# Two mixture-of-experts layers on one core: row fetches issued two experts ahead, parameter pieces queued behind them, gathers ahead of additions

## The chip, the cores and the metric

The kernel runs on one core of a Trainium2 chip. The metric is device microseconds (us) of one execution, and the figure that counts is the median of several executions. The engines are TensorE (PE, with its weight loads as PEld), VectorE (DVE), ScalarE (ACT), GpSimd (POOL) and SyncE (SP). Each has its own queue of instructions and works through it in order. SP, ACT and POOL also issue DMAs, and an issue is an instruction of their queue.

## The reference, cut to what matters

Two layers are computed over 512 tokens of 1024 numbers. Each layer has a mixer and then a mixture of 16 experts of which every token takes two. For every expert the tokens that chose it are collected, and with x those rows:

```python
hb = jax.nn.silu(xb @ w1[e]) * (xb @ w3[e])
return hb @ w2[e]
...
ys = ys * buf_gate[:, None]
out = jax.ops.segment_sum(ys, buf_tok, num_segments=T + 1)[:T]
```

The second layer's mixer has a state-space part (S5). Its small parameters go through exponentials, sines, cosines and a complex division before they are used; that work depends on nothing in the first layer, so it can be done while the first layer's experts run.

## The kernel before

Every float32 product is made as three products of a split operand: `split_half` (L335) takes a weight piece of 128x1024, ACT copies it to a rounded high part `wh` (L342) and DVE subtracts to get the low part `wl` (L343). PE then multiplies high by high, high by low and low by high (`mm3`, L346, lines 348 to 350). There are four buffers for `wh` and four for `wl` (L136), so that the splits run at most four ahead of PE.

`moe` (L1308) loops over the experts e = 0 to 15 (L1357). One turn of the loop holds, in this order of tracing: the products with W1 of expert e, the products with W2 of expert e - 1, the transposes of the rows of expert e + 1 (L1389), the products with W3 of expert e, and `expert_mid` of expert e (L1396), which applies the activation and transposes again. Each of the three weights is 4 MB and comes in four loads of 1 MB on SP, into a ring of buffers whose keys stand in `order`. In the first layer three keys leave that ring from expert 4 on (L1358 to 1359): the two `sx` buffers take the next layer's S5 parameters and `wx` gives its space to the work tiles of their preparation. When the preparation is over, `wx` goes back to the ring (L1405 to 1407).

The rows of experts 0 and 1 are gathered by products. Those of experts 2 to 15 are fetched by an indirect DMA from DRAM, issued on POOL: `fetch` (L1172, the DMA at L1174). At L1370 the rows of expert e + 1 are fetched in turn e, and they are transposed by PE in that same turn at L1256. The tile `xr` with the rows, and the transposed `hx` tiles, come from one ring of eight buffers.

The preparation of the S5 parameters is the generator `s5_params` (L479). In the first layer it is called with POOL as its engine and `two` = 1, at the end of turn 4 (`PREP`, L39, L1397 to 1400), after four small loads on the ACT queue (`s5_loads`, L459). Each `next` at L1403 traces the operations up to the next `yield`, at the end of one turn; there are nine yields for `two` = 1, so that the last operations are traced at the end of turn 13. One operation of it is a reciprocal on DVE (L545); all others are on POOL. `issue_after(ins)` sets only an order of issue: what the block traces on the engine of `ins` stands behind `ins` in that engine's queue. `self.mid` holds an ACT and a DVE instruction (L1258 and L1259), so the two `issue_after` at L1402 bind none of the POOL operations. The order within a queue is otherwise set by a planner when the kernel is built: it goes through the instructions by priority (by default the order of tracing, `high_priority` moves a block forward) and takes those that it holds to be ready, by its own estimate of when buffers and operands are there.

After the last expert `collect` (L1445) brings each token's two expert outputs together. For each of four groups of 128 tokens it issues two indirect gathers on POOL (L1452), into a buffer of the weight ring that is free again, and adds the two (L1457): the first 512 columns on DVE, the other 512 on POOL. `combine` (L1533) adds the sums to the accumulators by a product with the identity (L1543), beside the products for the last two experts' rows (`add_known`, L1432, and L1545). The fifth free buffer serves the last normalisation's scales (L268) or a scratch tile.

Of the kernel before, what the change touches and what calls it, by code (L numbers as in the profile page):

```python
# [21 lines left out]
NT = T // P  # L22
D = 1024
KD = D // P
DEPTH = 2
NE = 16
# [97 lines left out]
class Kernel:  # L124
# [354 lines left out]
    def s5_params(self, sp, sm, V, two):  # L479
# [4 lines left out]
        t = lambda nm, n=8: sp.tile([P, n], F32, name=nm, tag=nm)  # L484
# [11 lines left out]
        xm = t("xm", 64)  # L496
        V.tensor_tensor(v3(xm, 8), x[:, :, None].to_broadcast([P, 8, 8]),
                        mult[:, None, 0:8].to_broadcast([P, 8, 8]), OP.mult)
        mag = v3(self.poly_exp(sp, xm, 64, V), 8)
        at = 8 * NP * 16  # L500
        mag8 = self.s5c[:, at:at + 8]
# [8 lines left out]
        r = t("r", N)  # L510
        self.stt(V, r, k, -c1, af, OP.mult, OP.add)
        self.stt(V, r, k, -c2, r, OP.mult, OP.add, sp)
        V.tensor_scalar(r, r, 0.25, None, OP.mult)
        if two == 2:
            yield
        x2, s, cm = t("x2", N), t("s", N), t("cm", N)
        V.tensor_tensor(x2, r, r, OP.mult)
        V.tensor_scalar(s, x2, 1.0 / 362880, None, OP.mult)
        for f in (-1.0 / 5040, 1.0 / 120, -1.0 / 6):
            self.stt(V, s, s, f, x2, OP.add, OP.mult)  # L520
        self.stt(V, s, s, 1.0, r, OP.add, OP.mult)
        V.tensor_scalar(cm, x2, -1.0 / 3628800, None, OP.mult)
        for f in (1.0 / 40320, -1.0 / 720, 1.0 / 24, -0.5):
            self.stt(V, cm, cm, f, x2, OP.add, OP.mult)
        u = t("x2", N)
        for _ in range(2):
            self.stt(V, u, cm, 1.0, s, OP.add, OP.mult)
            self.stt(V, cm, s, -2.0, s, OP.mult, OP.mult)
            V.tensor_scalar(s, u, 2.0, None, OP.mult)
# [5 lines left out]
        V.tensor_tensor(L[:, 0], L[:, 0], mag, OP.add)  # L535
        V.tensor_tensor(L[:, 1], mag, v3(s, NT_)[:, :, 0:8], OP.mult)
        V.tensor_scalar(L[:, 2], L[:, 1], -1.0, None, OP.mult)
        l1, li = t("l1"), L[:, 1, :, 0]
        V.tensor_scalar(l1, L[:, 0, :, 0], -1.0, None, OP.add)
        d0, d1, n0, n1 = t("d0"), t("d1"), t("n0"), t("n1")  # L540
# [26 lines left out]
        for h in range(4):  # L567
# [3 lines left out]
            c = [cx[r][:, hs, 0:1, :].to_broadcast([P, *f]) for r in range(2)]  # L571
# [599 lines left out]

    def fetch(self, r, e):  # L1172
        t = self.keep.tile([P, D], F32, tag="hx", name="xr", bufs=8)[0:CAP]
        self.nc.gpsimd.indirect_dma_start(out=t, out_offset=None, in_=self.x_dram[:, :],  # L1174
                                          in_offset=bass.IndirectOffsetOnAxis(ap=r["idx"][e], axis=0))
        return t

    def places(self, r, pool):
# [129 lines left out]
    def moe(self, l, lg, nb, rs):  # L1308
        tc, nc, a = self.tc, self.nc, self.a
        W1, W3, W2 = (a[n][l] for n in ("moe_w1", "moe_w3", "moe_w2"))  # L1310
        Y = self.y_dram
        with tc.high_priority():
            self.keep_awake(WARM, self.asked)
            r = self.route(lg, self.hi)
        with self.pool("mw") as mw, ExitStack() as spare:
            self.wx = spare.enter_context(self.pool("wx"))

            def mk(e):
                def load(w, u):
                    key = order.pop(0)  # L1320
                    order.append(key)
                    return self.load(w[e, u * 256:(u + 1) * 256, :].rearrange("(k p) f -> p k f", p=P), (2, 1024),
                                     *slot(key))
                return load

            def slot(key):
                if key == "wx":
                    return self.wx, 1
                return (self.sx[int(key[2])], 1) if key[:2] == "sx" else bufs[key]
            bufs = dict(mr=(self.mr, 2), raw=(self.raw, 2), rows=(self.rows, 3))  # L1330
            order = ORDER.split()
# [22 lines left out]
                    self.gathered((ps[k][:, 0:256], ps[k][:, 256:]), nxt, k, 2, P)  # L1354
            pend = prep = None
            y = []
            for e in range(NE):  # L1357
                if e == PREP and l + 1 < self.layers:  # L1358
                    order[:] = [k for k in order if k[1] != "x"]
                if e == 1:  # L1360
                    with tc.issue_after(self.mid[1]):
                        self.places(r, self.hi)
                g = max(i for i, (a, n) in enumerate(GROUPS) if e >= a)
                at = e - GROUPS[g][0]
                if g == 0:
                    x = [[t[k // 4][:, k % 4, at * P:at * P + CAP] for k in range(KD)] for t in nxt]
                else:
                    x = cur
                if 0 < e < NE - 1:
                    xr = self.fetch(r, e + 1)  # L1370
                with ExitStack() as after:
                    if e == 0:
                        after.enter_context(tc.issue_after(r["dv"]))
                        after.enter_context(tc.issue_after(r["ex"]))
                    a1 = self.expert_in(W1, x, mk(e), ("pj", "pj"), ready if e == 0 else ())
                self.calm = False
                if e == 0:
                    with tc.issue_after(self.chosen):
                        self.gates(r, self.hi)
                        self.slots(mw, r, 0)  # L1380
                if e == NE - 1:
                    half = self.expert_out(mw, W2, pend, mk(e - 1), None, range(2))
                elif pend is not None:
                    y13 = self.keep.tile([P, D], F32, tag="hx", name="y", bufs=8) if e == NE - 2 else None
                    self.expert_out(mw, W2, pend, mk(e - 1), Y[(e - 1) * CAP:e * CAP, :], y=y13, gate=r["gate"][e - 1])
                if at == 0 and e < NE - 2:
                    A = self.slots(mw, r, g + 1)
                if 0 < e < NE - 1:
                    cur = self.transpose_split(xr, self.hx(KD * CAP), self.hx(KD * CAP), "zo", False)  # L1389
                if e == NE - 2:  # L1390
                    self.rest(A, r, mw)
                    self.overflow(l, r, mw, Y, y13[:, 0:T])
                a3 = self.expert_in(W3, x, mk(e), ("b", "b"))
                if e == NE - 1:
                    self.expert_out(mw, W2, pend, mk(e - 1), lambda ps: y.append(self.last_y(ps, 0)), range(2, 4), half)
                pend = self.expert_mid(mw, a1, a3)  # L1396
                if e == PREP and l + 1 < self.layers:  # L1397
                    spare.close()
                    sp = spare.enter_context(self.pool("s5p"))
                    prep = self.s5_params(sp, self.s5_loads(l + 1), nc.gpsimd, 1)  # L1400
                if prep:
                    with tc.issue_after(self.mid[0]), tc.issue_after(self.mid[1]):  # L1402
                        done = next(prep, 0) == 0  # L1403
                    if done:
                        prep = spare.close()  # L1405
                        self.wx = spare.enter_context(self.pool("wx"))
                        order.append("wx")
            self.cmb = []
            for c in range(NT - 1):
                self.cmb.append([self.bank(("pj", "b", "oz"[n])[c], "cmb") for n in range(2)])  # L1410
# [34 lines left out]
    def collect(self, r, Y, slots):  # L1445
        nc, tc = self.nc, self.tc
        self.acc = []
        ts = [pool.tile([P, 2048], F32, tag="raw", name="yg", bufs=n) for pool, n in slots]
        for c in range(NT):
            yg = ts[c][:, 0:D], ts[c][:, D:]  # L1450
            for j in range(2):
                nc.gpsimd.indirect_dma_start(out=yg[j], out_offset=None, in_=Y[:, :],  # L1452
                                             in_offset=bass.IndirectOffsetOnAxis(ap=r["pos"][:, j, c:c + 1], axis=0))
            with tc.issue_after(self.cut[1]):
                for i, eng in enumerate((nc.vector, nc.gpsimd)):
                    sl = slice(i * 512, (i + 1) * 512)
                    eng.tensor_tensor(yg[0][:, sl], yg[1][:, sl], yg[0][:, sl], OP.add)  # L1457
            self.acc.append(yg[0])
            self.rt[c] = yg[1]
# [143 lines left out]
```

## Time and profile before

| | us |
|---|---|
| median of 3 runs | 2251.75 |
| lowest and highest run | 2241.91, 2252.71 |
| the profiled execution | 2255.18 |
| its span, first to last instruction | 2253.4 |
| busy PE | 2120.9 (94%) |
| busy DVE | 1532.0 (68%) |
| busy ACT | 1229.7 (55%) |
| busy POOL | 445.4 (20%) |

The mean granted TensorE clock over the span is 0.965. The experts of the first layer run from about 505 to 1125 us of the span, those of the second from about 1638 to 2231 us. A busy PE is not a PE at its peak: matmuls are pipelined, and a product of 512 columns follows the one before it after about 0.23 us where its own row shows about 0.39 us. The time 2255.18 is that of the execution that the trace shows; times worked out from its rows are set against it, and it stands 3.43 us above the median.

### The profile page before, as it was taken

To read this page: it belongs to the slowest core of one execution; us is meant where nothing else is said; L and a number is where in the kernel's file an instruction comes from. 1 tells how busy PE (TensorE), PEld (TensorE's weight loads), DVE (VectorE), ACT (ScalarE), POOL (GpSimd) and SP (SyncE) were. 2 spreads that over 40 slices of the span, in tenths; PEclk is the share of its full clock that TensorE was granted. 3 is DMA by queue.
4 is the path that set the end of the run, shared out by engine and by line. 5 is a ranking of instruction groups with operands and counts; after the bars stand their busy time and mean duration, and the time that the engine had idled before them with its cause. 6 is when DMAs were issued, how large, how long until landed. Compare 5 with 4: busy or idle time off the path is not lost. (4 is left out here: it accounts for less than half of the span.)

```text
span 2253.4 us, 27509 instructions
## 1 busy us (share of the span) xinstructions
PE 2120.9 (94%) x10180; PEld 1564.4 (69%) x10181; DVE 1532.0 (68%) x1986; ACT 1229.7 (55%) x1548; POOL 445.4 (20%) x535
## 2 busy tenths in 40 slices
PE   7899999989993999998999999999899999999987
PEld 5678778876772666665667686888777776666654
DVE  8453533379993888887763435433699998888877
ACT  3333123237883777876643331223378887777763
POOL 5310231130069010000260101511310000000004
PEclk9999999999997999999999889999999999999999
DMA  6121365339995899998831112453289999999973
GB/s 195 46 74 52 105 206 179 118 124 349 373 344 185 319 360 380 367 378 319 319 124 57 39 64 64 165 182 122 103 320 386 385 389 351 380 366 382 367 302 125
DMA packets 192461, 533.16 MB, mean 237 GB/s; under 512 B 18545, under 2 KB 72433, under 8 KB 192306
## 3 DMA queue, kind: packets, MB, share of 16 engines
q1 hardware_dynamic: 173312, 476.69, 57.2%
q0 software_dynamic: 8032, 28.84, 3.8%
q10 hardware_dynamic: 10962, 25.67, 3.4%
q8 instruction: 84, 1.38, 0.2%
q14 instruction: 71, 0.58, 0.1%
HBM read 501.14 MB, written 27.00 MB: 234 GB/s over the span
## 5 line engine op out<-in xcount | busy, mean ns | idle before, releaser
L343 DVE TENSOR_TENSOR wl<-raw,wh 128x1024 fp32r<-128x1024 f32 x850 | 1026.6, 1242 | 392.0 <-ACT wh L342 366.8
L342 ACT CAST wh<-raw 128x1024 fp32r<-128x1024 f32 x872 | 895.8, 1050 | 426.3 <-PE e L350 150.1
L349 PE MATMUL e<-wl,hx 128*96 128x512 f32 x1024 | 408.2, 399 | 7.1 <-DVE wl L343 7.1
L350 PE MATMUL e<-wh,hx 128*96 128x512 f32 x1024 | 407.8, 398 | 0.0
L348 PE MATMUL e<-wh,hx 128*96 128x512 f32 x1024 | 383.6, 398 | 11.5 <-PEq L1480 11.3
L348 PE MATMUL pjf<-hx,wh 128*128 128x512 f32 x608 | 244.4, 402 | 4.5 <-DVE v L215 4.5
L350 PE MATMUL pjf<-hx,wl 128*128 128x512 f32 x608 | 243.7, 401 | 3.0 <-DVE wl L343 3.0
L349 PE MATMUL pjf<-hx,wh 128*128 128x512 f32 x608 | 244.5, 402 | 0.5 <-DVE hx L216 0.4
L349 PEld LDWEIGHTS e<-wl,hx 128*96 128x96 f32 x1024 | 166.9, 163 | 81.2 <-DVE wl L343 14.9
L348 PEld LDWEIGHTS e<-wh,hx 128*96 128x96 f32 x1024 | 166.7, 163 | 80.3 <-issue 12.5
L350 PEld LDWEIGHTS e<-wh,hx 128*96 128x96 f32 x1024 | 166.9, 163 | 66.5
L349 PE MATMUL e<-wl,gh 128*96 128x512 f32 x512 | 203.0, 396 | 5.0 <-DVE wl L343 4.2
L350 PE MATMUL e<-wh,gl 128*96 128x512 f32 x512 | 201.2, 394 | 2.6 <-DVE gl L1259 2.6
L348 PE MATMUL e<-wh,gh 128*96 128x512 f32 x512 | 180.2, 394 | 0.0
L1174 POOL DMA_INDIRECT xr<-xd,idx x28 | 43.2, 1543 | 675.5 <-PE tx L1256 498.4
L348 PEld LDWEIGHTS pjf<-hx,wh 128*128 128x128 f32 x608 | 115.6, 190 | 33.1 <-DVE v L215 5.7
L350 PEld LDWEIGHTS pjf<-hx,wl 128*128 128x128 f32 x608 | 115.5, 190 | 29.9 <-DVE wl L343 3.4
L349 PEld LDWEIGHTS pjf<-hx,wh 128*128 128x128 f32 x608 | 115.4, 190 | 28.9 <-DVE hx L216 1.6
L349 PEld LDWEIGHTS e<-wl,gh 128*96 128x96 f32 x512 | 82.6, 161 | 44.7 <-DVE wl L343 12.1
L350 PEld LDWEIGHTS e<-wh,gl 128*96 128x96 f32 x512 | 82.5, 161 | 36.2 <-DVE gl L1259 3.5
L348 PEld LDWEIGHTS e<-wh,gh 128*96 128x96 f32 x512 | 82.5, 161 | 35.3
L949 POOL TENSOR_TENSOR mg<-mg,gsg 128x512 f32<-128x512 f32 x32 | 42.8, 1342 | 212.2 <-DVE gsg L948 187.9
(500 smaller groups left out, 2787.0 us busy)
## 6 DMA issues: line engine op xcount, KB each, us to landing
raw<-in_moe_w_dram SPq DMA_DIRECT2D x384, 1024.0 KB, 7.5
raw<-in_w_in_dram SPq DMA_DIRECT2D x44, 1024.0 KB, 5.3
yd<-y ACTq DMA_DIRECT2D x28, 384.0 KB, 6.0
raw<-in_w_out_dram SPq DMA_DIRECT2D x8, 1024.0 KB, 5.5
yd<-zr ACTq DMA_DIRECT2D x14, 384.0 KB, 4.4
row<-hd POOLq DMA_DIRECT2D x8, 512.0 KB, 7.4
rawu<-in_w_up_c_dram SPq DMA_DIRECT2D x8, 512.0 KB, 3.4
xd<-row POOLq DMA_DIRECT2D x8, 512.0 KB, 3.1
```

Of the source, the lines that this page charges most:

```text
L342: self.cut = (nc.scalar.copy(hv, v).ins, (eng or nc.vector).tensor_tensor(lv, v, hv.bitcast(F32), OP.subtract).ins)
L343: (eng or nc.vector).tensor_tensor(lv, v, hv.bitcast(F32), OP.subtract).ins)
L348: mm(out, lh, rh, start=start, stop=False)
L349: mm(out, lh, rl, start=False, stop=False)
L350: mm(out, ll, rh, start=False, stop=stop)
L949: nc.gpsimd.tensor_tensor(mg[m], mg[m], sg, OP.add)
L1174: self.nc.gpsimd.indirect_dma_start(out=t, out_offset=None, in_=self.x_dram[:, :], in_offset=bass.IndirectOffsetOnAxis(ap=r["idx"][e], axi ...
```

## The change

`fetch` now keeps its DMA instruction in `self.fetched`. It is called at the end of the transposes of turn e, under `high_priority`, for expert e + 2, where before it was called at the head of turn e for expert e + 1. The preparation gets more yields for `two` = 1 (fifteen in place of nine), and `step` is called twice in a turn, after the W2 products and at the end, so that the last piece is traced in the middle of turn 12. What a step traces on POOL is queued behind the latest fetch in place of the two `mid` instructions, and its DVE reciprocal is bound to nothing. In `collect` all eight gathers are traced before the first addition. The yield that used to be taken for `two` = 2 alone is now taken for both, and the preparation of the first layer (`two` = 2, on DVE) yields where it did.

```diff
--- before.py
+++ after.py
@@ -496,6 +496,8 @@
         xm = t("xm", 64)
         V.tensor_tensor(v3(xm, 8), x[:, :, None].to_broadcast([P, 8, 8]),
                         mult[:, None, 0:8].to_broadcast([P, 8, 8]), OP.mult)
+        if two == 1:
+            yield
         mag = v3(self.poly_exp(sp, xm, 64, V), 8)
         at = 8 * NP * 16
         mag8 = self.s5c[:, at:at + 8]
@@ -511,19 +513,22 @@
         self.stt(V, r, k, -c1, af, OP.mult, OP.add)
         self.stt(V, r, k, -c2, r, OP.mult, OP.add, sp)
         V.tensor_scalar(r, r, 0.25, None, OP.mult)
-        if two == 2:
-            yield
+        yield
         x2, s, cm = t("x2", N), t("s", N), t("cm", N)
         V.tensor_tensor(x2, r, r, OP.mult)
         V.tensor_scalar(s, x2, 1.0 / 362880, None, OP.mult)
         for f in (-1.0 / 5040, 1.0 / 120, -1.0 / 6):
             self.stt(V, s, s, f, x2, OP.add, OP.mult)
         self.stt(V, s, s, 1.0, r, OP.add, OP.mult)
+        if two == 1:
+            yield
         V.tensor_scalar(cm, x2, -1.0 / 3628800, None, OP.mult)
         for f in (1.0 / 40320, -1.0 / 720, 1.0 / 24, -0.5):
             self.stt(V, cm, cm, f, x2, OP.add, OP.mult)
         u = t("x2", N)
         for _ in range(2):
+            if two == 1:
+                yield
             self.stt(V, u, cm, 1.0, s, OP.add, OP.mult)
             self.stt(V, cm, s, -2.0, s, OP.mult, OP.mult)
             V.tensor_scalar(s, u, 2.0, None, OP.mult)
@@ -535,6 +540,8 @@
         V.tensor_tensor(L[:, 0], L[:, 0], mag, OP.add)
         V.tensor_tensor(L[:, 1], mag, v3(s, NT_)[:, :, 0:8], OP.mult)
         V.tensor_scalar(L[:, 2], L[:, 1], -1.0, None, OP.mult)
+        if two == 1:
+            yield
         l1, li = t("l1"), L[:, 1, :, 0]
         V.tensor_scalar(l1, L[:, 0, :, 0], -1.0, None, OP.add)
         d0, d1, n0, n1 = t("d0"), t("d1"), t("n0"), t("n1")
@@ -1171,8 +1178,9 @@
 
     def fetch(self, r, e):
         t = self.keep.tile([P, D], F32, tag="hx", name="xr", bufs=8)[0:CAP]
-        self.nc.gpsimd.indirect_dma_start(out=t, out_offset=None, in_=self.x_dram[:, :],
-                                          in_offset=bass.IndirectOffsetOnAxis(ap=r["idx"][e], axis=0))
+        at = bass.IndirectOffsetOnAxis(ap=r["idx"][e], axis=0)
+        self.fetched = self.nc.gpsimd.indirect_dma_start(out=t, out_offset=None, in_=self.x_dram[:, :],
+                                                         in_offset=at).ins
         return t
 
     def places(self, r, pool):
@@ -1354,6 +1362,17 @@
                     self.gathered((ps[k][:, 0:256], ps[k][:, 256:]), nxt, k, 2, P)
             pend = prep = None
             y = []
+
+            def step():
+                nonlocal prep
+                if prep is None:
+                    return
+                with tc.issue_after(self.fetched):
+                    done = next(prep, 0) == 0
+                if done:
+                    prep = spare.close()
+                    self.wx = spare.enter_context(self.pool("wx"))
+                    order.append("wx")
             for e in range(NE):
                 if e == PREP and l + 1 < self.layers:
                     order[:] = [k for k in order if k[1] != "x"]
@@ -1366,8 +1385,6 @@
                     x = [[t[k // 4][:, k % 4, at * P:at * P + CAP] for k in range(KD)] for t in nxt]
                 else:
                     x = cur
-                if 0 < e < NE - 1:
-                    xr = self.fetch(r, e + 1)
                 with ExitStack() as after:
                     if e == 0:
                         after.enter_context(tc.issue_after(r["dv"]))
@@ -1383,10 +1400,14 @@
                 elif pend is not None:
                     y13 = self.keep.tile([P, D], F32, tag="hx", name="y", bufs=8) if e == NE - 2 else None
                     self.expert_out(mw, W2, pend, mk(e - 1), Y[(e - 1) * CAP:e * CAP, :], y=y13, gate=r["gate"][e - 1])
+                step()
                 if at == 0 and e < NE - 2:
                     A = self.slots(mw, r, g + 1)
                 if 0 < e < NE - 1:
                     cur = self.transpose_split(xr, self.hx(KD * CAP), self.hx(KD * CAP), "zo", False)
+                if e < NE - 2:
+                    with tc.high_priority():
+                        xr = self.fetch(r, e + 2)
                 if e == NE - 2:
                     self.rest(A, r, mw)
                     self.overflow(l, r, mw, Y, y13[:, 0:T])
@@ -1398,13 +1419,7 @@
                     spare.close()
                     sp = spare.enter_context(self.pool("s5p"))
                     prep = self.s5_params(sp, self.s5_loads(l + 1), nc.gpsimd, 1)
-                if prep:
-                    with tc.issue_after(self.mid[0]), tc.issue_after(self.mid[1]):
-                        done = next(prep, 0) == 0
-                    if done:
-                        prep = spare.close()
-                        self.wx = spare.enter_context(self.pool("wx"))
-                        order.append("wx")
+                step()
             self.cmb = []
             for c in range(NT - 1):
                 self.cmb.append([self.bank(("pj", "b", "oz"[n])[c], "cmb") for n in range(2)])
@@ -1446,11 +1461,12 @@
         nc, tc = self.nc, self.tc
         self.acc = []
         ts = [pool.tile([P, 2048], F32, tag="raw", name="yg", bufs=n) for pool, n in slots]
-        for c in range(NT):
-            yg = ts[c][:, 0:D], ts[c][:, D:]
+        ygs = [(t[:, 0:D], t[:, D:]) for t in ts]
+        for c, yg in enumerate(ygs):
             for j in range(2):
                 nc.gpsimd.indirect_dma_start(out=yg[j], out_offset=None, in_=Y[:, :],
                                              in_offset=bass.IndirectOffsetOnAxis(ap=r["pos"][:, j, c:c + 1], axis=0))
+        for c, yg in enumerate(ygs):
             with tc.issue_after(self.cut[1]):
                 for i, eng in enumerate((nc.vector, nc.gpsimd)):
                     sl = slice(i * 512, (i + 1) * 512)
```

## Rows read from the trace of the kernel before

**Rows 1.** The page, span in 40 slices: the granted TensorE clock in tenths.
```profile
PEclk9999999999997999999999889999999999999999
```

**Rows 2.** Waits of PE: who waited for whom, us in total, times, longest.
```profile
PE tx L1256 <- DMA xr<-xd,idx: 37.8, 1, 37.8
...
PE cmb L1543 <- POOL yg L1457: 8.8, 2, 5.4
```

**Rows 3.** Timeline of POOL, first layer, 597 to 790 us: start, length, operation, idle before.
```profile
597.69 2.17 POOL L1174 DMA_INDIRECT xr<-xd,idx  x1 [32.64 <-PE tx L1256]
637.87 0.28 POOL L443 TENSOR_SCALAR pe_xc<-small 128x8 f32<-128x8 f32 x1 [38.02 <-DMA small<-in_small_dram]
...
708.79 0.19 POOL L502 COPY s5c<-pe_o 128x8 f32<-128x8 f32 x1
...
729.33 0.53 POOL L580 TENSOR_SCALAR s5c<-s5c 128x128 f32<-128x128 f32 x1
730.03 1.02 POOL L1174 DMA_INDIRECT xr<-xd,idx  x1 [0.16 <-issue]
...
790.02 1.07 POOL L551 TENSOR_TENSOR zr<-n,d 128x8 f32<-128x8 f32 x1 [47.16 <-DVE d L545]
```

**Rows 4.** Line L1174 over the whole span: fetches from issue to landing.
```profile
DMA to landing us min/median/max: 4.0/8.1/11.2
```

**Rows 5.** Stretches of the first layer: busy us of each engine, PEclk, DMA share.
```profile
core 0: us, PE busy (x) PEld busy (x) DVE busy (x) ACT busy (x) POOL busy (x), PEclk, DMA share, GB/s
637.80:696.00 58.20, 58.20 (x273) 41.03 (x271) 54.37 (x53) 47.33 (x54) 54.70 (x57) 1.00 1.01 370
696.00:735.00 39.00, 1.24 (x15) 1.18 (x14) 3.58 (x4) 1.75 (x3) 34.81 (x72) 0.56 0.28 103
735.00:770.00 35.00, 35.00 (x154) 24.52 (x153) 29.03 (x30) 25.52 (x28) 0.91 (x1) 0.95 0.83 299
840.00:875.00 35.00, 34.12 (x158) 23.65 (x157) 30.19 (x31) 27.07 (x32) 1.28 (x1) 1.00 1.00 379
```

**Rows 6.** Transposes of fetched rows, experts 5, 7, 15, then 5, 15 of layer two.
```profile
L1256 PE MATMUL tx<-cs,xr x8: 244/246/247, 661.1 to 661.7; 96*128 96x96 f32 x8
...
L1256 PE MATMUL tx<-cs,xr x8: 243/246/247, 770.8 to 771.4; 96*128 96x96 f32 x8
...
L1256 PE MATMUL tx<-cs,xr x8: 243/244/246, 1041.5 to 1047.6; 96*128 96x96 f32 x8
...
L1256 PE MATMUL tx<-cs,xr x8: 244/246/247, 1794.5 to 1795.1; 96*128 96x96 f32 x8
...
L1256 PE MATMUL tx<-cs,xr x4: 244/246/248, 2134.8 to 2137.8; 96*128 96x96 f32 x4
```

**Rows 7.** Groups of DVE: splits at 637 to 696, then at 1731 to 1790 us.
```profile
L343 DVE TENSOR_TENSOR wl<-raw,wh 128x1024 fp32r<-128x1024 f32 x42 | 51.3, 1230 | 4.0 <-ACT wh L342 3.1
...
L343 DVE TENSOR_TENSOR wl<-raw,wh 128x1024 fp32r<-128x1024 f32 x42 | 50.9, 1222 | 4.1 <-ACT wh L342 3.6 <-DMA raw<-in_moe_w_dram 0.2
```

**Rows 8.** Timeline of POOL at the end of each layer: gathers and additions.
```profile
1112.42 7.30 POOL L1457 TENSOR_TENSOR yg<-yg 128x512 f32<-128x512 f32 x1 [5.24 <-DMA yg<-yd,pos]
...
1132.73 0.93 POOL L1452 DMA_INDIRECT yg<-yd,pos  x1 [0.31 <-issue]
...
2202.85 8.72 POOL L1452 DMA_INDIRECT yg<-yd,pos  x1 [0.15 <-issue]
...
2216.99 1.26 POOL L1457 TENSOR_TENSOR yg<-yg 128x512 f32<-128x512 f32 x1 [4.16 <-DMA yg<-yd,pos]
...
2222.15 0.94 POOL L1452 DMA_INDIRECT yg<-yd,pos  x1 [0.30 <-issue]
```

**Rows 9.** Timeline of PE at the end of each layer: the products that waited.
```profile
1128.10 1.22 PE L1543 MATMUL cmb<-yg,cs 128*128 128x512 f32 x1 [5.37 <-POOL yg L1457]
...
2218.30 1.13 PE L1543 MATMUL cmb<-yg,cs 128*128 128x512 f32 x2 [3.39 <-POOL yg L1457]
```

**Rows 10.** Timeline of DVE at 789.7 us: the reciprocal between two splits.
```profile
789.74 0.19 DVE L545 RECIPROCAL d<-d 128x8 f32<-128x8 f32 x1
```

## The prediction

> **What bounds the kernel now.** I read the whole page first. TensorE is busy for 94% of the span, so time is gained only where PE stands, and the row of the granted clock has one slice of 7 in the first layer's experts [rows 1]. Next I asked for PE's waits: one wait of 37.8 us, of the row transposes for an indirect DMA, is far longer than any other, and it occurs once in 28 fetches; the second to note is 8.8 us in two waits for additions on POOL [rows 2]. Then I read POOL's timeline around the long wait [rows 3]. POOL issues the fetch for expert 5 at 597.69, waits until 637.87 for the S5 loads, and runs preparation without a break to 729.86. Only then comes the fetch for expert 6, at 730.03. PE needed these rows at 696.4, since it went on at 734.20 after its 37.8 us. The fetch's buffer had long been free: in this layer a fetch otherwise goes right behind the transposes one expert earlier, which were those of expert 5, at 661.1 [rows 6]. So the block on POOL made it late, not memory, and the DMA share of 0.28 in the stretch says the weights were waiting too [rows 5].
>
> The second layer has the same experts and no preparation; it is the cleanest comparison at hand. From the transposes of expert 5's rows to those of expert 15's it takes 2134.8 - 1794.5 = 340.3 us, and the first layer 1041.5 - 661.1 = 380.4 us [rows 6]. The difference, 40.1 us, is what one block on POOL costs.
>
> **The fetches.** Fourteen fetches per layer stay fourteen; they move one expert ahead on POOL's queue, past two preparation pieces each, and no queue gets more DMAs. Fetch 6 is now traced in turn 4, ahead of the preparation, which must queue behind it. Its wait of 37.8 us goes. With it goes the clock's fall: while PE stood the granted clock was 0.56, and over the next 35 us it was 0.95 against 1.00 later [rows 5], in all 35 x 0.05 = 1.75 us of PE's work. Sum: 39.5 us, against 40.1 by the comparison of the layers.
>
> What is late next? Without the wait expert 7's transposes come at 770.8 - 39.5 = 731.3 [rows 6]. Fetch 7 can have two pieces ahead of it, the first two. These end with the copy at 708.79, and in the kernel before operations of later pieces ran among them [rows 3], so they end no later now. Fetch 7 then issues by 709 and lands 8.1 us later, 11.2 at worst [rows 4]: by 721, 10 us early. The pieces after it have about 20 operations or fewer between fetches; at 54.70 us for 57 operations, 0.96 us each beside busy splits [rows 5], that is under 20 us of an expert's 34 us (340.3 / 10). I cost them at nothing; if that cover went, each us beyond it would be a us of PE.
>
> The preparation's work itself, some 125 operations, is the same and now lies beside PE for its whole length. Does it slow the splits? DVE's split took 1230 ns with POOL's block beside it and 1222 ns in the second layer without [rows 7]; 8 ns on 42 splits is 0.3 us, and PE was busy for all 58.20 us of that stretch [rows 5]. So I take nothing. The other way round POOL does pay: 0.96 us an operation beside the splits, 34.81 / 72 = 0.48 us while PE and DVE stood [rows 5]. The Trainium skill says more (SBUF — State Buffer, "SBUF: two separate sides"): a DVE operation with two SBUF inputs and a GpSimd operation exclude each other for the whole instruction, whichever starts first. By that rule the splits should lose too, up to 125 x 0.48 = 60 us of DVE over eight experts, an estimate; by the rows it is POOL alone that waits, and the sum stays.
>
> `wx` returns to the ring one and a half turns earlier. More room ahead can only help; the smaller ring gives the first layer no later expert that is slower (from expert 7 to 15, 270.7 / 8 = 33.8 us each, the second layer's 34.0) [rows 6], so I take nothing.
>
> **The reciprocal.** It loses its order behind `mid` and can stand earlier in DVE's queue, where it waits for POOL's operations of the piece before it, which in turn stand behind the fetch for expert 9. Behind the reciprocal in DVE's queue are the splits, and PE runs on four of these: 34 / 24 = 1.4 us each, 5.6 us. Before, it cost 0.19 us between two splits [rows 10], and POOL waited 47.16 us for it, which cost nothing [rows 3]. No row shows DVE waiting for it. From below it costs nothing; it can't gain. From above: the two pieces behind that fetch have 15 operations, 15 x 0.96 = 14.4 us, less PE's 5.6: 9 us. I take 1, near the lower end, since the three products that it needs depend on the loads alone and are the first that POOL finds ready.
>
> **The gathers.** PE stood 5.37 us in the first layer and 3.39 in the second for POOL's addition of the second token group [rows 9], which came behind the first addition, stretched from some 1.26 us to 7.30 in the first layer, and behind a gather issue of 8.72 us in the second [rows 8]. With the gathers ahead, the second group's data is there sooner and both waits can go: from above 8.8 us of gain. From below: if POOL holds to all eight gathers first, the first two additions stand behind the last gather, whose buffer is freed by the last weights. That was issued by 1133.66 in the first layer and by 2223.09 in the second [rows 8]; with two additions of 1.26 us each, PE would go on at 1136.2 instead of 1128.1 and 2225.6 instead of 2218.3, a loss of 8.1 + 7.3 us. Both gathers were late because additions stood ahead of them, so the lower end is too dark. I take 3 us of gain for the first layer, whose buffers also come free earlier with `wx` back in the ring at another place, and 1 for the second, where no buffer changes.
>
> The Trainium skill names a trap here (SBUF — State Buffer, "SBUF: two separate sides"): a DMA issued on GpSimd can't get its descriptors written while DVE holds the shared port. The 8.72 us issue, beside splits, agrees with it; other issues of 0.93 us beside splits do not [rows 8]. By that rule the second layer's later gathers would be stretched again and its gain would be nil.
>
> **Sum.** 37.8 + 1.75 - 1 + 3 + 1 = 42.5 us. From the profiled execution's 2255.2 that gives 2212.7; the median stands 3.4 lower, so 2209.
>
> **Rivals.**
> (a) The reciprocal and the gathers both turn out near their bad ends: 39.5 - 9 - 15.4 = 15 us are left, 2237; half of that, 2224, is likelier. For it: in-order queues, no row that shows either. Against: one stall of each kind only.
> (b) The change doesn't do what it says: a fetch is late all the same, since POOL's pieces stand ahead of fetch 7 with only 10 us to spare. If the loads for the preparation land 10 + x later, x is lost; at the 38 us of now, 2252, no change. Against: the loads come in turn 4 as before, and the order behind a fetch is fixed.
> (c) Slower, by one mechanism: the reciprocal on DVE. If the planner puts it at the place where the whole preparation could begin, and POOL gets to its operands only at the end of some 92 us (637.87 to 729.86) [rows 3], DVE stands 92 us and PE 92 - 5.6 = 86: 2252 - 39.5 + 86 = 2298. It decides from a wait of 45 us (39.5 + 5.6), where all the gain is gone. Against: its operands need the loads only, and stand behind one fetch, not behind all pieces.
>
> **Chances.** Forecast 0.80, with 2198 to 2220 as its own span; (a) 0.10, still faster; (b) 0.06, of which 0.05 ends within 0.5% and 0.01 faster; (c) 0.04. A measurement of this kernel tells about 0.5%, 11 us, from no change. So faster 0.91, same 0.05, slower 0.04. For the range: the lower end is all gains, 40.1 + 8.8 = 48.9 below 2251.75, 2203, and 5 more because the runs before spread 10 us downwards; the upper end takes in the larger part of (a), 2232. That leaves out (b), (c) and the rest of (a).
>
> **What would show it.** The fetch row of PE's waits gone, and no slice of 7 in the clock row before 1000 us; from expert 5's transposes to expert 15's some 340 us in the first layer; POOL's preparation in clumps between fetches over about seven experts; the waits of L1543 shorter than 5.37 and 3.39 us. The prediction is wrong if a transpose still waits for `xr`, if DVE shows a wait of tens of us before L545, or if the split row rises above 1.23 us with PE waiting on L343.

## The result, and the profile after

The kernel after takes 2215.64 us, the median of 8 runs (2207.34 to 2233.51), the kernel before 2252.16 us in 8 runs beside it (2237.64 to 2255.02). The ratio is 0.987, with a 95% interval of 0.9832 to 0.9908, wholly below 1: the kernel is 1.3% faster, inside the range, 6.6 us above the forecast. The profiled execution took 2214.86 us, with a span of 2213.1 and a mean clock of 0.976 (before 2255.18, 2253.4 and 0.965).

The long wait for the fetched rows [rows 2] is gone from PE's waits, which now begin so:

```profile
PE e L349 <- DVE wl L343: 14.7, 31, 2.0
...
PE cmb L1559 <- POOL yg L1473: 7.6, 2, 6.1
```

The first row is the wait for a VectorE split: in the kernel before 11.3 us in 26 waits, the longest 0.6; now 14.7 us, with one of 2.0. The clock row has lost its slice of 7 [rows 1]:

```profile
PEclk9988999999999999999999999999999999999999
```

POOL's timeline (start, length, operation, idle before) shows fetch 6 ahead of the preparation, and fetches 7 and 8 between its pieces, where one block stood before [rows 3]:

```profile
633.70 0.91 POOL L1182 DMA_INDIRECT xr<-xd,idx  x1 [27.83 <-PE tx L1264]
643.96 0.28 POOL L443 TENSOR_SCALAR pe_xc<-small 128x8 f32<-128x8 f32 x1 [9.35 <-DMA small<-in_small_dram]
...
695.02 1.07 POOL L504 COPY s5c<-pe_o 128x8 f32<-128x8 f32 x1
696.26 2.04 POOL L1182 DMA_INDIRECT xr<-xd,idx  x1 [0.17 <-issue]
...
724.68 2.02 POOL L1182 DMA_INDIRECT xr<-xd,idx  x1 [0.16 <-PE e L350]
```

The row transposes of experts 5 and 15, in the first layer and then in the second, answer to [rows 6]:

```profile
L1264 PE MATMUL tx<-cs,xr x8: 244/246/247, 667.2 to 667.8; 96*128 96x96 f32 x8
...
L1264 PE MATMUL tx<-cs,xr x8: 243/244/246, 1013.6 to 1019.7; 96*128 96x96 f32 x8
...
L1264 PE MATMUL tx<-cs,xr x8: 244/246/247, 1755.5 to 1756.1; 96*128 96x96 f32 x8
...
L1264 PE MATMUL tx<-cs,xr x8: 243/244/246, 2095.7 to 2101.9; 96*128 96x96 f32 x8
```

From expert 5 to expert 15, which I call the stretch, the first layer takes 346.4 us (380.4 before) and the second 340.2, as before. So 34.0 us came back and 6.1 are still lost (346.36 - 340.23 by the timeline's hundredths). The lag over the second layer is 0.3 us at expert 9, 2.7 at 10, 5.0 at 11, 6.1 at 12, and then stays: it arises between 798 us, where expert 9's transposes start, and 912, where expert 12's do.

The layers' ends: from expert 15's transposes to the next layer's first product it is 119.3 us (117.1 before), and from those of the second layer to the last instruction 117.4 (118.6). PE's waits at the first combine answer to [rows 9]:

```profile
1099.97 2.08 PE L1559 MATMUL cmb<-yg,cs 128*128 128x512 f32 x2 [6.09 <-POOL yg L1473]
...
2177.94 1.12 PE L1559 MATMUL cmb<-yg,cs 128*128 128x512 f32 x2 [1.49 <-POOL yg L1473]
```

The span fell by 40.3 us: 34.0 in the stretch, 1.3 at the second layer's end, less 2.2 at the first layer's. Nearly all of the other 7.2 lies in the two mixers, which the change doesn't touch: the first is 6.0 us longer (its clock from 100 to 200 us is 0.86, was 0.93), the second 13.5 shorter (0.98, was 0.95). Among all the kernels run, expert 2's transposes come anywhere from 555.2 to 565.1 us, with nothing altered ahead of them. What the change itself does is thus 32 to 33 us (the second layer's 1.3 may not be its own), and single runs are compared below by the stretch, which in the second layer is 340.1 to 340.4 us in every kernel run.

### The profile page after: what moved, and what is told of

Read it like the earlier page. It is cut to its first block, busy times and chain, and to the rows that moved or that the text cites. A ratio compares the mean times of both kernels' runs of the same rounds, so it can differ in the third digit from the quotient of the medians.

```text
span 2213.1 us, 27508 instructions
## 1 busy us (share of the span) xinstructions
PE 2114.7 (96%) x10178; PEld 1557.3 (70%) x10181; DVE 1545.0 (70%) x1986; ACT 1230.4 (56%) x1548; POOL 505.0 (23%) x535
## 5 line engine op out<-in xcount | busy, mean ns | idle before, releaser
L343 DVE TENSOR_TENSOR wl<-raw,wh 128x1024 fp32r<-128x1024 f32 x850 | 1042.3, 1261 | 345.5 <-ACT wh L342 310.6
```

Source lines behind the costliest of these rows:

```text
L343: (eng or nc.vector).tensor_tensor(lv, v, hv.bitcast(F32), OP.subtract).ins)
```

## The experiments

All edits are to the kernel after, except where said. The whole time is a median for before, after, best and chain_late, and one run for the others.

| kernel | stretch, layer 1 | end, layer 1 | whole us |
|---|---|---|---|
| before | 380.4 | 117.1 | 2252.2 |
| after | 346.4 | 119.3 | 2215.6 |
| undo_queue | 381.3 | 120.0 | 2243.7 |
| undo_early | 346.1 | 119.3 | 2213.4 |
| undo_pieces | 349.0 | 118.4 | 2215.9 |
| queue_alone | 358.2 | 117.6 | 2232.5 |
| undo_gathers | 347.0 | 119.7 | 2218.4 |
| wide_on_vector | 342.1 | 122.3 | 2217.8 |
| wide_twice | 350.7 | 119.6 | 2229.5 |
| wide_cut | 358.6 | 119.7 | 2227.6 |
| cut_chain | 340.9 | 119.2 | 2220.1 |
| wx_late | 347.4 | 117.1 | 2215.1 |
| best | 342.0 | 116.9 | 2207.0 |
| chain_late | 341.0 | 117.4 | 2208.0 |

### Which part carries the gain

**undo_queue.**
```diff
-                with tc.issue_after(self.fetched):
+                with tc.issue_after(self.mid[0]), tc.issue_after(self.mid[1]):
                     done = next(prep, 0) == 0
```


> The kernel after with the pieces held behind the two middle steps, as before, and not behind the last fetch; fetches still two experts ahead, pieces still small. POOL is then given fetches 2 to 5, the whole preparation (some 125 operations), and fetch 6 behind it. Theory QUEUE (what costs is the fetch standing behind the preparation on POOL, wherever the code writes it): fetch 6 near 730 us, a wait of TensorE of 30 to 40 us for it, a stretch of 376 to 384. Rival AHEAD (two experts of distance are what carries the gain): 346 to 350.

381.3 us: the whole stall is back, with fetches two ahead and small pieces. PE's waits, then POOL's timeline:

```profile
PE tx L1264 <- DMA xr<-xd,idx: 37.9, 1, 37.9
```
```profile
596.82 2.16 POOL L1182 DMA_INDIRECT xr<-xd,idx  x1 [32.65 <-PE tx L1264]
...
729.15 1.02 POOL L1182 DMA_INDIRECT xr<-xd,idx  x1 [0.16 <-issue]
```

The code asks for fetch 6 an expert earlier, but POOL is handed it behind the block all the same. QUEUE holds, AHEAD falls.

**undo_early.**
```diff
+                if 0 < e < NE - 1:
+                    xr = self.fetch(r, e + 1)
                 with ExitStack() as after:
...
-                if e < NE - 2:
-                    with tc.high_priority():
-                        xr = self.fetch(r, e + 2)
```


> The kernel after with each fetch issued one expert ahead, at the head of the turn, as before; the pieces stay small and stay behind the last fetch. POOL then has fetches 2 to 5, a piece, fetch 6, a piece, fetch 7 and so on: fetch 6 near 667 us for transposes at 702, fetch 7 near 705 for 737, fetch 8 near 731 for 758. QUEUE: all land in time, a stretch of 346 to 348. AHEAD: fetches late again by several us each, 355 or more.

346.1 us, and no wait for a fetch: those of experts 6, 7 and 8 go out at 667.48, 707.45 and 733.07 us, as expected. With small pieces that queue behind the fetch, one expert of distance is enough.

**undo_pieces.** The added `yield`s are taken out, and `step()` stands only at the end of a turn.


> The kernel after with the parameters in their old, larger pieces, one a turn; the fetches stay two experts ahead, and the pieces behind them. POOL then has fetches 2 to 6, some 51 operations, fetch 7, 47 operations, fetch 8. At 1.05 to 1.25 us an operation (as in the trace after, beside busy splits) fetch 8 is issued near 757 us where the kernel after issues it at 724.7, and expert 8's transposes stood at 758.2. Theory PIECES (the small pieces are needed): TensorE waits 4 to 8 us for fetch 8, a stretch of 350 to 354. Rival: two experts ahead is margin enough by itself, 346.

349.0 us, 1 us under the range. The mechanism is there: fetch 8 at 752.87 us behind the 47 operations, and a wait of 2.2 us, the only one for rows. Two experts of distance almost cover a large piece; small pieces are worth 2.6 us beside them (349.0 - 346.4).

**queue_alone.** The kernel before with one edit (its gathers are in the order of after, which moves nothing, see undo_gathers):
```diff
-                    with tc.issue_after(self.mid[0]), tc.issue_after(self.mid[1]):
+                    with tc.issue_after(self.fetched):
```


> The kernel before with one thing changed: the pieces of the parameters stand behind the last fetch on POOL, and not behind the two middle steps. Fetches one expert ahead and pieces large, as before. POOL then has fetches 2 to 5, some 51 operations, fetch 6, 47 operations, fetch 7, fetch 8. Fetch 6 is issued near 697 us for transposes at 702, fetch 7 near 757 for 737 (or as much later as fetch 6 came late). If small pieces and two experts of distance each are enough, but one of them is needed, TensorE waits 0 to 6 us for fetch 6 and 18 to 28 us for fetch 7: a stretch of 360 to 376. If the place in the queue is all that counts: 346 to 350.

358.2 us, under the range, and for a reason that I hadn't named: PE has no wait for rows here. Three views of it, VectorE, POOL and PE:

```profile
664.22 0.55 DVE L1260 TENSOR_TENSOR hx<-tx,hx 128x384 fp32r<-128x384 f32 x1
677.30 0.20 DVE L545 RECIPROCAL d<-d 128x8 f32<-128x8 f32 x1 [12.53 <-POOL d L543]
```
```profile
674.73 1.01 POOL L1175 DMA_INDIRECT xr<-xd,idx  x1 [0.53 <-issue]
...
677.07 0.20 POOL L543 TENSOR_TENSOR d<-d,d 128x8 f32<-128x8 f32 x1
```
```profile
678.75 0.74 PE L349 MATMUL e<-wl,hx 128*96 128x512 f32 x1 [10.52 <-DVE wl L343]
```

The reciprocal came up in VectorE's queue at 664.77 us, and its operand `d` stood on POOL behind the whole first piece and fetch 6. VectorE stood 12.53 us with splits behind it, and PE 10.52. This is rival (c) of the prediction, at a smaller size. In the kernel after the reciprocal has a `yield` ahead of it and runs at 766.24 us between two splits, without a wait. The order behind the last fetch thus brings 22.2 of the 34 us alone (380.4 - 358.2); small pieces bring the rest (undo_early), and the greater distance in their place nearly as much (undo_pieces).

**undo_gathers.** The hunk in the collecting function is taken back.


> The kernel after with the combine gathers and additions written in the order of before (each block's gathers ahead of its own additions only). The order that each engine is given is then the same as in the kernel after, so this part of the change does nothing by itself: a stretch of 346.4 give or take 0.3, the wait of TensorE at the first layer's combine near 6.1 us, the second layer's near 1.5 us, and the whole time within what runs of one kernel differ by. If the edit does something after all, the ends differ: 5.4 and 3.4 us, as before.

347.0 us, waits of 6.01 and 1.40 at the two combines: the kernel after again, its stretch 0.6 us longer with the same order of operations on POOL, VectorE and ScalarE. So 0.3 was too narrow a margin, and this part of the change does nothing.

### Where the 6 us go

The wide operations of the preparation (128x128 and 128x256) run on POOL from 803 to 886 us, which is where the lag arises. In the kernel before the twenty-four 128x256 products fell into the stall. POOL and VectorE after:

```profile
811.27 0.62 POOL L583 TENSOR_TENSOR small<-small,s5c 128x256 f32<-128x256 f32 x1
811.85 0.61 POOL L584 TENSOR_TENSOR cw<-s5c 128x256 f32<-128x256 f32 x1
812.43 0.61 POOL L583 TENSOR_TENSOR s5c<-small,s5c 128x256 f32<-128x256 f32 x1
813.01 0.63 POOL L585 TENSOR_TENSOR small<-small,cw 128x256 f32<-128x256 f32 x1
813.72 1.49 POOL L584 TENSOR_TENSOR cw<-s5c 128x256 f32<-128x256 f32 x1
...
838.61 1.63 POOL L584 TENSOR_TENSOR cw<-s5c 128x256 f32<-128x256 f32 x1
840.21 1.60 POOL L583 TENSOR_TENSOR s5c<-small,s5c 128x256 f32<-128x256 f32 x1
```
```profile
802.82 8.16 DVE L343 TENSOR_TENSOR wl<-raw,wh 128x1024 fp32r<-128x1024 f32 x6
811.90 11.74 DVE L343 TENSOR_TENSOR wl<-raw,wh 128x1024 fp32r<-128x1024 f32 x8 [0.92 <-ACT wh L342]
...
838.42 23.55 DVE L343 TENSOR_TENSOR wl<-raw,wh 128x1024 fp32r<-128x1024 f32 x16 [0.27 <-ACT wh L342]
...
889.67 9.18 DVE L343 TENSOR_TENSOR wl<-raw,wh 128x1024 fp32r<-128x1024 f32 x8 [1.23 <-ACT wh L342]
```

A product alone takes 0.62 us, and beside busy splits 1.60: one product, one split, by turns. Six splits beside 128x128 operations take 8.16 / 6 = 1.36 us each, and sixteen from 838.42, eleven of them beside 128x256, 1.47 on average. With nothing on POOL beside them, eight in a row take 9.18 / 8 = 1.15 us each (a single row shows 1.22 [rows 7], since each split starts a little before the last has ended). TensorE uses one in 340.2 / 240 = 1.42 us, so only the widest reach it. PE's named waits for splits rose by only 3.4 us (14.7 - 11.3), since a product's row covers 0.39 us where the next one usually starts after 0.23, and hides short pauses. Counted from start to start, the pauses between the expert products of the stretch add up to some 6 us more than in the second layer.

**wide_on_vector.**
```diff
-        G = nc.gpsimd
+        G = nc.gpsimd if two == 2 else nc.vector
+        H = V if two == 2 else nc.vector
...
-        V.tensor_tensor(q[0], bn[:, 0], zrb, OP.mult)
+        H.tensor_tensor(q[0], bn[:, 0], zrb, OP.mult)
...
-                with tc.issue_after(self.fetched):
+                with tc.issue_after(self.fetched), tc.issue_after(self.mid[1]):
```


> The kernel after, with the thirty-one wide operations of the first layer's parameters (six 128x128 products, twenty-four 128x256 products, one 128x128 scaling) on VectorE in place of POOL; nothing else moves. The measure is the stretch from expert 5's row transposes to expert 15's in the first layer: 380.4 us before, 346.4 after, 340.2 in the second layer, which has no parameters to prepare. Theory PORT (a wide POOL operation and a VectorE split hold each other off, and that is where the 6.1 us over the second layer come from): the splits go back from 1.57 to 1.69 us to 1.22 to 1.26 us, VectorE takes some 10 us of products into its 20% of idle time, and the stretch is 340.5 to 343. Rival PLACE (the 6 us come from the ring of weight buffers that the parameters' space takes away, or from their loads): 346 as before, or more, since VectorE has more to do.

342.1 us: 4.3 of the 6.1 are back. The last hunk moves one thing more, the reciprocal, to 829.18 us; VectorE has no wait before it. From 803 to 940 us 91 splits take 1220 ns on average, with 26 of the wide operations on VectorE among them, 420 ns for a 128x256. PORT holds.

**wide_twice.**
```diff
+                for _ in range(3 - two):
                     G.tensor_tensor(o, c[0], x0, OP.mult)
...
```


> The kernel after, with each of the twenty-four 128x256 POOL products of the first layer done twice in a row. PORT: each added product holds one more split for about 0.4 us (1.6 us in place of 1.22), of which about 0.24 us come through to TensorE, whose own pace is 1.38 us a piece: 24 x 0.24 = 5.8 us more, a stretch of 351 to 353. PLACE: the ring and the loads are as they were, 346.

350.7 us, 4.3 more (0.18 a product, where I had 0.24), just under the range, and far from PLACE.

**wide_cut.** The three lines of a product run four times, on quarters of 64 columns.


> The kernel after, with each 128x256 POOL product cut into four 128x64 ones (96 in place of 24): the same elements, in operations as narrow as those of the earlier pieces, beside which the splits took 1.21 to 1.26 us. PORT, if a split loses by the length of the one POOL operation that it meets: splits of about 1.25 us, below TensorE's 1.38 us a piece, and a stretch of 341 to 343, with the products spread over three times as many splits. If it is the POOL time in all that is lost: 346 or more. PLACE: 346.

358.6 us: a clear miss, and the most telling run. POOL, VectorE and PE:

```profile
840.54 1.27 POOL L590 TENSOR_TENSOR small<-small,cw 128x64 f32<-128x64 f32 x1
841.78 1.27 POOL L588 TENSOR_TENSOR small<-small,s5c 128x64 f32<-128x64 f32 x1
...
847.97 0.29 POOL L590 TENSOR_TENSOR small<-small,cw 128x64 f32<-128x64 f32 x1
848.22 0.28 POOL L588 TENSOR_TENSOR s5c<-small,s5c 128x64 f32<-128x64 f32 x1
...
856.93 0.28 POOL L589 TENSOR_TENSOR cw<-s5c 128x64 f32<-128x64 f32 x1
```
```profile
837.95 9.90 DVE L343 TENSOR_TENSOR wl<-raw,wh 128x1024 fp32r<-128x1024 f32 x8 [0.30 <-ACT wh L342]
849.69 13.43 DVE L343 TENSOR_TENSOR wl<-raw,wh 128x1024 fp32r<-128x1024 f32 x5 [1.83 <-ACT wh L342]
```
```profile
858.38 0.74 PE L349 MATMUL e<-wl,hx 128*96 128x512 f32 x1 [7.84 <-DVE wl L343]
```

While eight splits follow one another, each lets one product in between and takes 9.90 / 8 = 1.24 us: a narrow one costs 0.09 (1.24 - 1.15). At 847.85 VectorE has no next split for 1.83 us, since ScalarE's cast isn't there. From then on POOL's products follow every 0.25 us, each starting before the last has ended (0.28), and the split that comes at 849.69 isn't done before 858. PE stood 7.84 us here, and 5.80 in the same way at 812.73. So the length of one operation is not what counts. The rows suggest that the engine that has the turn keeps it while its next operation follows without a gap; POOL's time in all (96 x 0.28 = 27 us, was 24 x 0.62 = 15) could explain the stretch as well, and the next run tells them apart. The first four products of the kernel after (811.27 to 813.64) are such a run, and PE's wait of 2.0 us (until 814.77) stands behind it.

**cut_chain.**
```diff
+                    s0, s1 = w[:, 0:1, 0:4], w[:, 0:1, 4:8]
+                    G.tensor_tensor(s0, cs[0], lx[0], OP.mult)
+                    G.tensor_tensor(s1, cs[1], lx[1], OP.mult)
+                    G.tensor_tensor(o[:, at[0], at[1]], s0, s1, OP.subtract)
```


> The kernel with the cut products (96 of 128x64), but both products of a step go to one small scratch that the step's subtraction reads, so that each step of three operations has to follow the step ahead of it: the POOL operations come one behind another with a gap, where those of the cut products ran back to back at 0.25 us. Theory HOLD (the engine that has the port keeps it as long as its next operation follows without a gap, and a split that comes meanwhile waits for the whole run of operations): no run is longer than three operations of 0.25 us, TensorE's longest wait for a split falls from 7.8 us to under 1 us, the operations take 1.0 to 1.3 us each beside busy splits, and the stretch of experts 5 to 15 falls from 358.6 to 341 to 345. Rival TOTAL (the number of POOL operations, or their time in all, is what costs): 355 to 360 again.

340.9 us, 0.7 over the second layer. The same 96 narrow operations, put into a chain, cost 17.7 us less than unchained. Of these, 63 take over 1 us each, by turns with the splits. ScalarE's cast is late here too, by 1.81 us, and POOL goes on alone in that gap, but eight splits then follow in 9.95 us, where in wide_cut five took 13.43. POOL, then VectorE:

```profile
839.75 1.16 POOL L588 TENSOR_TENSOR cw<-small,s5c 128x64 f32<-128x64 f32 x1
...
842.22 1.19 POOL L590 TENSOR_TENSOR small<-cw 128x64 f32<-128x64 f32 x1
843.48 1.16 POOL L588 TENSOR_TENSOR cw<-small,s5c 128x64 f32<-128x64 f32 x1
...
848.24 0.29 POOL L588 TENSOR_TENSOR cw<-small,s5c 128x64 f32<-128x64 f32 x1
848.49 0.29 POOL L589 TENSOR_TENSOR cw<-s5c 128x64 f32<-128x64 f32 x1
848.86 1.31 POOL L590 TENSOR_TENSOR s5c<-cw 128x64 f32<-128x64 f32 x1
```
```profile
848.77 9.95 DVE L343 TENSOR_TENSOR wl<-raw,wh 128x1024 fp32r<-128x1024 f32 x8 [1.81 <-ACT wh L342]
```

PE's longest wait for a split, 7.8 us unchained, is the 0.6 of the kernel before:

```profile
PE e L349 <- DVE wl L343: 12.1, 28, 0.6
```

TOTAL falls: the operations are as many as in wide_cut. What VectorE loses in all isn't the cost either: its splits took 1039.7 us here and 1042.3 in the kernel after (1026.6 before). HOLD is shown for POOL, in one state: after VectorE has missed a turn, POOL runs on, and a split that comes then waits until POOL pauses. In the chain a pause comes after two operations at the latest (848.78 to 848.86, and the split of 848.77 goes first). While both engines have work at every turn they alternate, though neither's rows show a gap, so HOLD as I worded it is too wide.

### The first layer's end, and the two best versions

**wx_late.**
```diff
                 if done:
                     prep = spare.close()
-                    self.wx = spare.enter_context(self.pool("wx"))
-                    order.append("wx")
...
                 step()
+                if e == NE - 3 and l + 1 < self.layers:
...
+                    self.wx = spare.enter_context(self.pool("wx"))
+                    order.append("wx")
```


> The kernel after, with the weight buffer that the parameters' space gives back put into the ring only at the end of turn 13, as before, and not when the last piece is done. Theory RING (the other order of the ring's buffers sets the order of gathers and additions at the first layer's end, and that costs the 2.2 us between expert 15's transposes and the next layer's first product: 119.3 us after, 117.1 before): 117.0 to 117.6 us, and TensorE's wait at the first combine 5.4 us in place of 6.1. Rival: 119 as after, the 2.2 us being something else; the stretch of experts 5 to 15 stays at 346 by either, or is a little longer if the tenth buffer was of use.

117.1 us and a wait of 5.57, the stretch 1.0 us longer. RING holds for the end: where the buffer comes back into the ring's order decides whose buffer a gather must wait for, and POOL's order of gathers and additions is then that of the kernel before.

**best.** The edits of wide_on_vector and wx_late together.


> The kernel after with the thirty-one wide operations on VectorE and with the weight buffer put back into the ring only at the end of turn 13. From the two runs by themselves: the stretch of experts 5 to 15 in the first layer 342 us in place of 346.4, the first layer's end 117.1 in place of 119.3: 6 to 7 us off the kernel after, so 2206 to 2212 us, and 0.977 to 0.983 of the time before. If VectorE's part and the ring's part get in each other's way (the run with the products on VectorE had 122.3 us at the first layer's end), 2213 to 2218, no better than after.

2206.98 us (2195.95 to 2209.89 in 6 runs), a ratio of 0.9795 (0.9762 to 0.9828) to the kernel before, with 342.0 and 116.9 us. The 122.3 us that wide_on_vector had at the first layer's end, 3.0 more than the kernel after, are gone with the ring's place; there PE had stood 3.27 us for VectorE's `ywl`, 0.58 in the kernel after. The interval lies just below that of the kernel after; both beat the kernel before.

**chain_late.** The edits of cut_chain and wx_late together.


> The other remedy as a whole kernel: the products stay on POOL, cut and chained as in the run before, and the weight buffer goes back into the ring at the end of turn 13. By the stretches: experts 5 to 15 in 340.9 us and the first layer's end in 117, some 1 us less than with the products on VectorE (342.0 and 116.9), which is below what whole runs can tell apart: 2203 to 2211 us, 0.976 to 0.982 of the time before. If chained products at the first layer's end still disturb the gathers there, 119 for the end and 2206 to 2214.

2208.04 us (2201.53 to 2215.22 in 5 runs), a ratio of 0.9786 (0.9762 to 0.981), with 341.0 and 117.4 us. The two can't be told apart.

## Why the prediction was right, and which terms were off

**The fetches, 37.8 us: right.** The wait is gone, fetch 7 went out at 696.26 where I allowed 709, and undo_queue brings all of it back by the queue's order alone. My wording gave the credit to "one expert ahead on POOL's queue"; undo_early shows that the distance isn't needed.

**The clock, 1.75 us: right in size.** The first layer lost 40.1 us to the second before, 37.8 in the wait; 2.3 are left for it.

**The pieces beside the splits, nothing: wrong, 6.1 us.** The step that failed is "by the rows it is POOL alone that waits, and the sum stays". The rows were those beside operations of 8 to 104 columns [rows 7]; the 128x256 ones ran in the stall of the kernel before, where hardly a split was there to be held up [rows 5]. I read the cost of the narrow half of the work as that of all of it. The measured cost is 6.1 us in the stretch; 4.3 go with the wide operations moved to VectorE, 5.5 with narrow ones in a chain. That the Trainium skill's rule (SBUF — State Buffer, "SBUF: two separate sides": the two engines' operations exclude each other for the whole instruction, whichever starts first) speaks against the change was right in direction: products and splits go by turns, 1.60 us for a product of 0.62. Not all of it agrees: a split and a product one after the other would take 1.15 + 0.62 = 1.77 us, and in wide_cut it was not one instruction but a whole run of them that held a split off. The bound of 60 us of VectorE, my estimate, was too high: its splits took 15.7 us more than in the kernel before (1042.3 - 1026.6), and 6.1 of these came through to TensorE.

**The reciprocal, -1: nothing, as its lower end had it.** It ran at 766.24 us without a wait. The mechanism that I feared is real: queue_alone has it, with 12.53 us on VectorE and 10.52 on PE, so that the splits made ahead covered 2.0 us there, and not the 5.6 of my sum.

**The gathers, +3 and +1: the first wrong in sign.** The first layer's end is 2.2 us longer. I wrote that its "buffers also come free earlier with `wx` back in the ring at another place"; wx_late shows that this place is what costs. The edit to the gathers moves nothing (undo_gathers). Two readings beside this term were wrong as well. The issue of 0.93 us at 1132.73 [rows 8] had no split beside it until 1133.62; only that of 0.94 us at 2222.15 had one, from 2222.40. And the trap that I took from the Trainium skill (SBUF — State Buffer, "SBUF: two separate sides") is told there of VectorE operations in a two-port mode; I left that condition out, and no run here shows the splits to be such. The second layer's 1.3 us isn't the change's either: its end takes 116.5 to 117.9 us in ten kernels, undo_gathers with the gathers of before among them (117.6), and 118.6 to 120.8 in four, the kernel before being one. What sets that is open.

**The sum.** Put right, it is 40.1 - 6.1 - 2.2 + 1.3 = 33.1 us where I had 42.5, or 31.8 without the 1.3 that isn't the change's. The median fell by 36.5; the mixers' clock differs between executions by more than the remainder. By these sums the median would be 2219.1 or 2220.4, at the upper end of my own span for the forecast, 2198 to 2220: that it held was luck in part.

**The rivals.** (b) didn't come. Half of (a), 2224, is near 2252 - 33 = 2219, but not by its causes: the reciprocal cost nothing, and the first layer's end 2.2 us by the ring's order and not by additions behind the last gather. (c) came only in queue_alone.

**The signs.** Fetch row, clock row and clumps came as named; so did the warning, a split row above 1.23 us with PE waiting on L343: the mean of all splits rose from 1242 to 1261 ns. The stretch of "some 340 us" was 346.4. Of the waits of L1543 (L1559 after) that were to be shorter, the second was (1.49 us for 3.39), the first was longer (6.09 for 5.37).

## What to carry to other kernels

Ask in which order each engine is handed its work, not where the code asks for it: fetching earlier did nothing until the filler work was ordered behind the fetch, and then, with small pieces, one expert of distance was enough. Work that ran inside a stall has no price in the trace once the stall goes: price it by rows in which the same shapes run beside the busy engine, or as unknown. Filler on POOL beside VectorE's splits did best here narrow and in a dependent chain (340.9 us); independent operations back to back held VectorE up for the whole run, and cutting them smaller without chaining them made it worse (358.6 for 346.4).

## What the hardware showed that I had not expected

Once POOL runs on alone, with operations that follow without a gap, it keeps VectorE out until it pauses. At a pitch of 0.25 us such a run stretched one split to over 8 us (849.69 to beyond 858 in wide_cut). The three holds that I looked at (splits of 806.03 and 849.69 in wide_cut, of 811.90 in the kernel after) all began where the next split was missing for a moment, 0.9 to 1.8 us behind ScalarE's cast.

A POOL operation let in between two consecutive splits costs the split less than its own length: 1.24 us a split beside products of 0.28 us, 1.36 beside 128x128 ones, 1.60 beside ones of 0.62, against 1.15 alone.

When VectorE lets POOL in is open. Mostly it is after each split, but in the kernel before the addition of 7.30 us (1112.42 to 1119.72) and the gather issue of 8.72 us (2202.85 to 2211.57) [rows 8] ended only after the last of the splits beside them, at 1118.56 and 2210.75:

```profile
1113.94 4.62 DVE L343 TENSOR_TENSOR wl<-raw,wh 128x1024 fp32r<-128x1024 f32 x4
...
2206.13 4.62 DVE L343 TENSOR_TENSOR wl<-raw,wh 128x1024 fp32r<-128x1024 f32 x4
```
